# A four-layer hybrid trunk on one core: the heads of its FFNs written out by hand through their second block, with the weight sums on VectorE, and the last products of differential attention shared out between the pieces that follow them

## The chip, the core and the metric

One core of a Trainium2 chip runs the whole program in one launch. The core has five engines with queues of their own: TensorE (PE in the profile, its weight loads PEld), VectorE (DVE), ScalarE (ACT), GpSimd (POOL) and SyncE (SP), and 16 DMA engines that all of them share. The metric is the time of one execution in microseconds (us). For the kernel before, three runs took 2422.5 to 2428.01 us, median 2423.11.

## The reference, cut to what matters

`x` has 512 tokens of 1024 numbers in float32. Four layers follow each other; each adds a mixer and then an FFN to `x`. The mixers are S5, GLA, differential attention and S5 again.

```
for layer in range(4):
    h = rmsnorm(x, norm_mix[layer]);  x = x + mixer[layer](h)
    h = rmsnorm(x, norm_ffn[layer])
    g, u = split(h @ w_gate_up[layer])        # 1024 -> 2 x 2816
    x = x + (silu(g) * u) @ w_down[layer]     # 2816 -> 1024
```

Differential attention ends in `o @ w_o`, a product of 512 x 1024 by 1024 x 1024, which is added to `x`.

## The kernel before, in words

**Products in three parts.** Each float32 operand is split into a high part, rounded to a form that TensorE reads quickly (`F32R`), and a low part, the rest. A product is three matmuls: high by high, high by low, low by high. The high part is a copy on ScalarE (line 279 for weights, 185 for activations) and the low part a subtraction on VectorE that waits for it (280 and 186). `Trunk.halves` (276 to 281) does both for a weight piece of 128 x 1024 and writes a tile `whl`, of which there are 5.

**FFN of layers 1, 2 and 3** (`Trunk.ffn` and `seven_block`). The 2816 hidden columns are cut into 11 blocks of 256. In a block, gate and up together are a 2 x 2 block product: two halves of the tokens by two halves of the 1024 inputs, times two halves of the inputs by (gate, up). It is done with seven products instead of eight, in Winograd's form. The left operands, called sides, are `11`, `12`, `22`, which are quarters of the activations, and `1`, `2`, `3`, `4`, sums and differences of them (`Sides.total`, 191 to 205). The right operands are quarters of the weights: `11` and `21` (gate), `22` (up), and sums: `1` is up plus gate of the first input half, `3` is up of both halves. These two sums are made by DMA: a load from SP's queue (534 or 273), and then a second, accumulating load from GpSimd's queue (537), which waits until the first has landed. Later, `22` and then `21` are added onto `1` in place (`added`, 593, and the beginning of `four`, 613): on GpSimd for blocks 0 and 1, on VectorE for the others.

Each product is 24 matmuls of 128 x 256 (line 508). The steps of a block are `one` (sides `11`, weights `11`), `two` (`12`, `21`), `five` (`1`, `1`), `six` (`2`, `1` + `22`), `seven` (`3`, `3`), `three` (`4`, `22`), `four` (`22`, `1` + `22` + `21`). `one`, `six`, `seven` and `four` accumulate in the same PSUM bank `a`, so each waits until the one before has been copied or subtracted out (572, 600, 604, 546); `five` and `three` share bank `c`, `two` has `d`. The outcome is `act`, silu(gate) times up, again split (629, 630).

**Normalisation.** The sides are taken from `x` times the gain; the factor 1/rms of each token comes later. `Left.take` (78 to 92) multiplies by the gain (86), squares on ScalarE (98), and appends a transposition to the list `pend`, which `flush` empties one call later. `put` (103) transposes on TensorE (107) and `keep` (188) copies out. `finish` (116) makes 1/rms, with a power on GpSimd (125); `diag`, `spread` and `rows` (128 to 142) make of it a tile `R` that has the factor of each token in every row.

**Room.** The four quarters of the activations lie in `F`. When the sides have been built, each quarter's room takes weights of blocks 2 and 3 (`freed`). Other rooms are three `slots`, the gain's tile, and two `lent` rooms for the first two blocks' `1`. A staged weight goes to `wst`, of which there are 3.

**The head.** The first two blocks (a and b below) overlap the building of the sides. `Trunk.hand` switches the scheduler off: what is emitted then stands in each engine's queue as written. In `ffn` the steps from `split("21")` of block 0 up to `six` of block 1 are written by hand; the rest (`seven`, `three`, `four` of blocks 0 and 1, and all from block 2 on) is ordered by the scheduler. The loads of a block come in the order `11`, `21`, `1`, `22`, `3`, and rooms are handed out first in, first out. SP's queue and GpSimd's queue run their DMAs in order: one that waits holds those behind it.

After block 3, block 7 and block 10 a product with `w_down` (`gemm_b`, 294 to 296) adds to `x`. In layer 2, when block 2's loads have been issued, `turn_x` (737 to 748) writes `x` to memory and reads it back in another order of tokens, from GpSimd's queue; its results in `act` are written in two pieces (`turn`).

**The end of differential attention** (`diff`, up to 1990). Its product with `w_o` is made in two halves of 512 columns. The first half (`last`) runs between the heads' softmax work. Of the second, token tiles 0 and 1 run in two banks up to their last input tile, then `last` is emptied, then these two are finished, and then tiles 2 and 3. Each finished tile is added to `x` (438) and handed to `take`; each `take` first puts out the transposition that the one before left.

## Time and profile before

| | |
|---|---|
| median of three runs | 2423.11 us (2422.5 to 2428.01) |
| the profiled execution | 2425.78 us, of which its span is 2424.1 us |
| instructions | 35200 |
| TensorE busy | 2282.2 us, 94% of the span |
| VectorE, ScalarE, GpSimd busy | 1495.5, 1070.4 and 329.8 us |
| memory read, written | 275.92 MB, 23.99 MB |

How to read the rows that follow in the prediction. A row of the order of events has start and length in us, engine, line, operation, written tile and read tiles, their shapes, a count when equal instructions were merged, and in brackets how long the engine had been idle before and what ended that. `SPq` and `POOLq` are the queues that issue DMAs. A row of stretches has the stretch, its length, busy time of PE, PEld, DVE, ACT and POOL with counts, the granted TensorE clock as a share of full speed, the busy share of the DMA engines, and GB/s. A row of DMA issues has the tile, the count, the KB of each and the us from issue to landing.

### The profile page before, as it was taken

What the parts mean: (1) busy time and instruction counts of PE and PEld (TensorE: products, weight loads), DVE (VectorE), ACT (ScalarE), POOL (GpSimd) and SP (SyncE); (2) the same over time, 40 slices, a digit from 0 to 9 for tenths busy, and PEclk for the clock granted to TensorE, in tenths of its full rate; (3) what the DMA queues carried; (4) which work ended last, traced back from release to release, by engine and by line L of the source; (5) the groups of instructions that cost most, each with busy time, mean ns of one, the idle gap of its engine ahead of it and who ended that gap; (6) DMA issues with size and microseconds to landing.
All of it is one profiled execution on the core that took longest, in us unless ns stands there. A gap on an engine that the chain in (4) does not pass through costs nothing. (4 is left out here: it accounts for less than half of the span.)

```text
span 2424.1 us, 35200 instructions
## 1 busy us (share of the span) xinstructions
PE 2282.2 (94%) x14054; PEld 1975.2 (81%) x14054; DVE 1495.5 (62%) x2276; ACT 1070.4 (44%) x1740; POOL 329.8 (14%) x366
## 2 busy tenths in 40 slices
PE   4799999999999998999999998899999799899997
PEld 3578888788877788898987886798989688899996
DVE  7764655555433477484754676875856874867674
ACT  4453435444352355252534675553533233544442
POOL 4330100210100021010002131310000210301000
PEclk9799999999999999999999999999999899999999
DMA  4124343544432258574335465585732645666621
GB/s 111 32 50 139 101 148 126 165 132 155 135 96 70 83 135 207 131 180 118 105 127 121 106 143 153 145 231 125 186 90 85 210 160 142 166 173 142 172 72 69
DMA packets 275503, 317.42 MB, mean 131 GB/s; under 512 B 45653, under 2 KB 214377, under 8 KB 274058
## 3 DMA queue, kind: packets, MB, share of 16 engines
q1 hardware_dynamic: 227210, 238.14, 31.7%
q0 software_dynamic: 48128, 77.02, 15.4%
q8 instruction: 111, 1.82, 0.3%
q14 instruction: 54, 0.44, 0.1%
HBM read 275.92 MB, written 23.99 MB: 124 GB/s over the span
## 5 line engine op out<-in xcount | busy, mean ns | idle before, releaser
L280 DVE TENSOR_TENSOR whl<-wst,whl 128x1024 fp32r<-128x1024 f32 x294 | 359.9, 1226 | 367.8 <-ACT whl L279 365.0
L279 ACT CAST whl<-wst 128x1024 fp32r<-128x1024 f32 x294 | 308.7, 1052 | 531.5 <-PE acc L296 352.7
L508 PE MATMUL a<-side,whl 128*128 128x256 f32 x2376 | 301.5, 285 | 33.9 <-ACT r L600 26.9
L508 PEld LDWEIGHTS a<-side,whl 128*128 128x128 f32 x2376 | 290.7, 195 | 36.8 <-ACT r L600 28.1
L296 PE MATMUL acc<-whl,act 128*128 128x512 f32 x704 | 277.3, 394 | 0.0
L295 PE MATMUL acc<-whl,act 128*128 128x512 f32 x704 | 276.0, 392 | 0.0
L294 PE MATMUL acc<-whl,act 128*128 128x512 f32 x704 | 275.5, 391 | 0.0
L508 PE MATMUL c<-side,whl 128*128 128x256 f32 x1584 | 191.9, 277 | 0.2 <-DVE whl L280 0.2
L508 PEld LDWEIGHTS c<-side,whl 128*128 128x128 f32 x1584 | 186.3, 188 | 0.4 <-DVE whl L280 0.4
L295 PEld LDWEIGHTS acc<-whl,act 128*128 128x128 f32 x704 | 132.2, 188 | 29.4
L294 PEld LDWEIGHTS acc<-whl,act 128*128 128x128 f32 x704 | 132.2, 188 | 29.4 <-issue 0.7
L296 PEld LDWEIGHTS acc<-whl,act 128*128 128x128 f32 x704 | 132.3, 188 | 26.9
L294 PE MATMUL any<-hT,whl 128*128 128x512 f32 x384 | 151.7, 395 | 0.0
L295 PE MATMUL any<-hT,whl 128*128 128x512 f32 x384 | 149.6, 390 | 0.0
L296 PE MATMUL any<-hT,whl 128*128 128x512 f32 x384 | 149.6, 390 | 0.0
L294 PE MATMUL acc<-whl,hT 128*128 128x512 f32 x352 | 144.3, 410 | 2.0 <-DVE ro L1784 1.3
L295 PE MATMUL acc<-whl,hT 128*128 128x512 f32 x352 | 139.2, 395 | 0.9 <-DVE whl L280 0.9
L296 PE MATMUL acc<-whl,hT 128*128 128x512 f32 x352 | 139.4, 396 | 0.0
L280 DVE TENSOR_TENSOR whl<-halves,whl 128x1024 fp32r<-128x1024 f32 x60 | 73.4, 1224 | 67.7 <-ACT whl L279 67.4
L295 PE MATMUL acc<-whl,zT 128*128 128x512 f32 x256 | 103.9, 406 | 5.2 <-DVE whl L280 5.2
L294 PE MATMUL acc<-whl,zT 128*128 128x512 f32 x256 | 103.1, 405 | 2.7 <-ACT zT L410 2.7
L296 PE MATMUL acc<-whl,zT 128*128 128x512 f32 x256 | 103.6, 406 | 1.2 <-DVE zT L411 1.2
(425 smaller groups left out, 4253.4 us busy)
## 6 DMA issues: line engine op xcount, KB each, us to landing
wst<-in_ffn_w_gate_up_dram SPq DMA_DIRECT2D x110, 512.0 KB, 3.9
wst<-in_ffn_w_down_dram SPq DMA_DIRECT2D x88, 512.0 KB, 3.9
halves<-in_ffn_w_gate_up_dram SPq DMA_DIRECT2D x42, 512.0 KB, 4.7
slot<-in_ffn_w_gate_up_dram SPq DMA_DIRECT2D x39, 512.0 KB, 4.4
wst<-in_ffn_w_gate_up_dram POOLq DMA_DIRECT2D x33, 512.0 KB, 6.3
wst<-in_s_w_glu_dram SPq DMA_DIRECT2D x32, 512.0 KB, 3.7
spill<-opsp POOLq DMA_DIRECT2D x8, 2048.0 KB, 8.8
wst<-in_gla_w_in_dram SPq DMA_DIRECT2D x24, 512.0 KB, 3.6
```

Of the source, the lines that this page charges most:

```text
L279: nc.scalar.copy(hl[:, 0], w[:])
L280: nc.vector.tensor_tensor(hl[:, 1], w[:], hl[:, 0].bitcast(F32), op=ALU.subtract)
L294: mm(out, lh, rh, start=first, stop=False)
L295: mm(out, lh, rl, start=False, stop=False)
L296: mm(out, ll, rh, start=False, stop=last)
L508: mm(o, hl[:, x, k, c], side[:, y, k], start=first and not (j or k or n), stop=k == 3 and n == 2, skip_group_check=True,)
```

## The change

1. In `ffn`, the whole of blocks 0 and 1 up to their last products is now written by hand, as a list of words in which `:a` and `:b` are steps of block 0 and 1, a trailing `a` or `b` belongs to a split, a sum, a high or a low part of that block, and words without are those of the sides. `seven`, `three` and `four` are cut into a product and what follows it (`_out`). Splits can be written as high part (ScalarE) and low part (VectorE) apart.
2. The sums of `22` and `21` onto `1` are on VectorE for all blocks.
3. The loads of blocks from 2 on come in the order `11`, `1`, `22`, `21`, `3`, and the rooms of the sides are handed out in a new order, mixed with the slots.
4. The square of the last token tile and half is a step of the list (`square`); `r2` of block 1 has a tile of its own.
5. At the end of `diff`, `take` no longer flushes (`lazy`); the eight transpositions, the two additions of tiles 0 and 1, and the two early weight pieces (`ahead`) are put between the products of token tiles 2 and 3. `hand_all` is called there and in `gemm_b`, just ahead of `ahead`, no longer inside it.

```diff
@@ Left.take
-        tr.flush(1 - d)
-        if d and self.early:
+        if not tr.lazy:
+            tr.flush(1 - d)
+        if d and self.early and t < NT - 1:
             self.square(t, d)
...
@@ seven_block
-        def added():
-            (nc.gpsimd if b < 2 else v).tensor_tensor(W["1"][:], W["1"][:], W["22"][:], op=ALU.add)
+        def add(name):
+            v.tensor_tensor(W["1"][:], W["1"][:], W[name][:], op=ALU.add)
+            done(name) if name == "21" else None
...
         def four():
-            (nc.gpsimd if b < 2 else v).tensor_tensor(W["1"][:], W["1"][:], W["21"][:], op=ALU.add)
-            done("21")
-            self.seven_product(A["22"], W["1"], bank["a"], False)
+            product("22", "1", bank["a"], False)
             done("1")
+
+        def four_out():
             g2 = T("g2")
             scaled(g2, bank["a"], 1)
...
@@ ffn, instead of the calls for f[0], f[1] and left, one by one
+            plan = """
+                split21a one:a split21b square flush one:b total1 one_out:a finish high1 low1 total2 split1a high2 low2
+                one_out:b two:a two:b split1b high3 two_out:a five:a add22a highSa two_out:b lowSa five_out:a five:b
+                add22b highSb diag lowSb low3 split3a six:a spread five_out:b rows six:b six_out:a split3b seven:a
+                six_out:b total4 split22a high4 low4 seven:b seven_out:a split22b three:a seven_out:b gate1:a gate1:b
+                high22 low22 three:b add21a highFa add21b lowFa highFb lowFb four:a four:b three_out:a three_out:b
+            """
...
             self.hand()
-            slots += left.freed() + [left.g[:].rearrange("p (k n) -> p k n", n=256)]
+            F = left.freed()
+            slots[:] = [F[0], F[1], slots[0], F[2], left.g[:].rearrange("p (k n) -> p k n", n=256), F[3]] + slots[1:]
...
                     if n > 1:
-                        b["direct"]()
-                        b["roomed"]()
-                        b["rest"]()
-                        b["summed"]()
+                        for w in ("direct", "room1", "room22", "room21", "summed"):
+                            b[w]()
...
@@ diff
+            self.lazy = True
             run(last)
-            nxt[0].ahead(1)
+            self.hand_all()
             evac = self.add_x(1, nxt[0])
             for t in range(2):
                 unit(t, KT - 1)
-                evac(t, banks[t])
+            one = lambda: self.pend.pop(0)()
+            between = {
+                2: {1: (one,), 3: (one, lambda: evac(0, banks[0])), 5: (one, lambda: evac(1, banks[1])), 7: (one,)},
+                3: {1: (one,), 3: (one, lambda: nxt[0].ahead(1)), 5: (one,)},
+            }
             for t in range(2, NT):
                 banks.append(self.acc())
-                if t == 3:
-                    nxt[0].ahead(1)
                 for k in range(KT):
                     unit(t, k)
+                    for f in between[t].get(k, ()):
+                        f()
                 evac(t, banks[t])
+                if t == 2:
+                    nxt[0].ahead(1)
+            self.lazy = False
```

More of the change, by code (lines that the diff above doesn't have):

```diff
@@ L631, in four @@
             return act
[L633 to L637 removed]
+        return {f.__name__: f for f in (
+            high, low, split, direct, room21, room1, room22, summed, one, one_out, two, two_out, gate1, five, five_out,
+            add, six, six_out, seven, seven_out, three, three_out, four, four_out,
+        )}
     def ffn(self, l, left, after=None, turn=False, aside=None):
```

144 lines of the change are left out of this document (71 added, 73 removed).

## The prediction

> **What bounds the kernel now.** I read the busy table first, then the time by stages, then the order of events on TensorE where a stage has holes. TensorE (PE) is busy for most of the span, so time can only be won where it waits or where its clock is low.
>
> ```profile
> PE 2282.2 (94%) x14054; PEld 1975.2 (81%) x14054; DVE 1495.5 (62%) x2276; ACT 1070.4 (44%) x1740; POOL 329.8 (14%) x366
> ...
> 880.48:955.65 75.17, 64.02 (x519) 63.05 (x518) 63.69 (x67) 39.69 (x52) 20.65 (x11) 0.95 0.68 168
> 955.65:1100.00 144.35, 144.35 (x1049) 135.89 (x1048) 99.83 (x110) 66.93 (x82) 11.58 (x9) 1.00 0.63 162
> 1526.00:1606.78 80.78, 67.52 (x520) 66.53 (x518) 67.02 (x72) 44.08 (x59) 23.40 (x15) 0.90 0.77 202
> 2059.62:2134.04 74.42, 64.74 (x519) 63.58 (x518) 64.07 (x66) 41.17 (x53) 20.70 (x11) 0.93 0.68 170
> ```
>
> The rows after the first are stretches: length, busy time of PE, weight load, DVE, ACT and POOL, granted clock, DMA share, GB/s. Three are the FFN heads of layers 1, 2 and 3, from the first product of block 0 to the first of block 3; 955.65:1100 is what follows in layer 1, where PE is never idle. So block 3 onwards is PE's own pace and the heads are not: in each, PE idles for about 10 to 13 us and the clock is 0.90 to 0.95. The change touches just these and the stretch before 1526.
>
> ```profile
> 909.31 3.01 PE L508 MATMUL a<-side,whl 128*128 128x256 f32 x24 [3.26 <-ACT r L600]
> 929.18 5.49 PE L508 MATMUL a<-side,whl 128*128 128x256 f32 x24 [6.11 <-ACT r L600]
> 955.65 3.02 PE L508 MATMUL a<-sides,whl 128*128 128x256 f32 x24
> 975.01 0.39 PE L294 MATMUL acc<-whl,act 128*128 128x512 f32 x1
> ```
>
> Start, length, operation, and in brackets the wait before it. These are the two largest waits of head 1, 9.4 of its 11.1 us of idle time (75.17 less 64.02). The seven products of block 3 run from 955.65 to 975.01, 2.77 us each. So the 21 products of a head need 58.2 of its 75.2 us.
>
> **Why it waits.**
>
> ```profile
> 890.24 1.22 DVE L280 TENSOR_TENSOR whl<-lent,whl 128x1024 fp32r<-128x1024 f32 x1
> 892.87 3.13 DVE L280 TENSOR_TENSOR whl<-lent,whl 128x1024 fp32r<-128x1024 f32 x1 [0.21 <-ACT whl L279]
> 895.92 0.67 DVE L579 TENSOR_TENSOR r<-r,d 128x512 f32<-128x512 f32 x1
> 896.52 3.05 DVE L280 TENSOR_TENSOR whl<-lent,whl 128x1024 fp32r<-128x1024 f32 x1
> ...
> 900.09 3.05 DVE L280 TENSOR_TENSOR whl<-lent,whl 128x1024 fp32r<-128x1024 f32 x1
> 903.06 3.50 DVE L186 TENSOR_TENSOR side<-s,side 128x512 fp32r<-128x512 f32 x2
> 891.53 3.38 POOL L593 TENSOR_TENSOR lent<-lent,slot 128x1024 f32<-128x1024 f32 x1 [5.07 <-DVE whl L280]
> 907.72 0.37 SPq L534 DMA_DIRECT2D halves<-in_ffn_w_gate_up_dram  x1
> 913.06 1.28 POOL L537 DMA_DIRECT2D halves<-in_ffn_w_gate_up_dram  x1 [1.94 <-DMA halves<-in_ffn_w_gate_up_dram]
> 925.08 1.05 ACT L279 CAST whl<-halves 128x1024 fp32r<-128x1024 f32 x1 [7.16 <-DMA halves<-in_ffn_w_gate_up_dram]
> ```
>
> Two causes. A low part costs DVE 1.22 us, but 3.05 to 3.50 beside GpSimd's four weight sums, which makes the 3.26 wait. And block 2's summed quarter is loaded into the last side to come free (907.72), added at 913.06 and read only at 925.08: that is the 6.11. Layer 2 repeats both, and the stretch of layer 3 is alike.
>
> ```profile
> 1554.80 4.37 PE L508 MATMUL a<-side,whl 128*128 128x256 f32 x24 [3.34 <-ACT r L600]
> 1574.80 5.43 PE L508 MATMUL a<-side,whl 128*128 128x256 f32 x24 [5.86 <-ACT r L600]
> 1601.49 5.49 PE L508 MATMUL a<-side,whl 128*128 128x256 f32 x24 [3.21 <-DVE r L604]
> 1562.96 25.41 DMA gain<-in_ffn_w_gate_up_dram
> xturn<-vall POOLq DMA_DIRECT2D x1, 2048.0 KB, 27.0
> 904.00:912.00 8.00, 4.74 (x41) 4.54 (x40) 8.00 (x7) 4.70 (x7) 3.32 (x2) 1.00 0.67 209
> 1553.00:1561.00 8.00, 6.21 (x40) 6.21 (x41) 8.00 (x9) 7.19 (x9) 3.02 (x4) 0.79 0.92 262
> 1600.00:1608.00 8.00, 6.51 (x33) 6.51 (x34) 7.11 (x9) 3.88 (x5) 1.29 (x1) 0.57 0.90 217
> ```
>
> Layer 2 has a third wait of 3.21 us: block 3's quarter lies in the gain's room and lands after 25.4 us, beside the turn of x (27.0). Waits also cost clock: around 1553 and 1600 it is 0.79 and 0.57, which is 1.7 and 3.4 us in 8; around 904, at an equal wait, it is 1.00.
>
> **The change part by part.** *Sums to VectorE.* Each head loses four GpSimd sums and gains four of 1.14 us on DVE (the pace of such pieces: 886.64 less 885.50 in the rows of L205 and L132, length 1.22). It loses 1.9, 1.8 and 1.8 us of blocked low parts and 2.2 in the two of 903.06 (1.3 when free, as two 512-wide pieces): 7.8 out, 4.6 in. DVE works 63.7 - 3.2 = 60.5 us in a head. GpSimd's queue then has only r and the accumulating DMAs, which no longer stand behind sums.
>
> *Order and rooms.* Block 2's summed quarter now goes into the first side to come free, after the second total (about 9 us into the head instead of 27), and nothing but r is ahead of its accumulation. By the rows above, 5.3 us for the load and 12 for the sum, it is there at about 26, and wanted at 46: the 6.11 and 5.86 waits lose this cause by 20 us. Block 3's quarter follows at 28 instead of 37 or later. SP is passed too: the two staged loads now stand ahead of the second side and wait for block 0's and 1's third quarter, at 23 to 25 us; the side behind them is free at 25, so this is free of charge.
>
> *What is late next.* I laid the new written order of PE, DVE and ACT with the paces of the rows, start to start: product 2.77, DVE 1.14 (1024 wide) and 0.60 (512: 895.92 to 896.52), ACT 0.95, 0.48 (a copy) and 0.53 (silu). A hand-over takes 0.14 (891.78 + 0.95 to 892.87), and 0.3 behind PE, whose product rows are 0.25 longer than their pace.
>
> ```profile
> 885.50 1.22 DVE L205 TENSOR_TENSOR halves<-halves 128x1024 f32<-128x1024 f32 x1
> 886.64 0.87 DVE L132 TENSOR_SCALAR diag<-ident,rcol 128x128 f32<-128x128 f32 x4
> 889.62 1.05 PE L138 MATMUL rows<-diag,ones 128*128 128x128 f32 x8
> 891.78 1.05 ACT L279 CAST whl<-lent 128x1024 fp32r<-128x1024 f32 x1
> 908.68 0.58 ACT L600 COPY r<-a 128x512 f32<-128x512 f32 x1
> 909.15 1.05 ACT L185 CAST side<-halves 128x1024 fp32r<-128x1024 f32 x1
> 910.11 0.63 ACT L547 ACTIVATE r<-r 128x512 f32<-128x512 f32 x1
> 910.64 1.04 ACT L279 CAST whl<-wst 128x1024 fp32r<-128x1024 f32 x1
> ```
>
> PE then runs twelve products, `one:a` to `three:b`, with transposes and row sums (1.2) and 0.4 for slower first products, without a wait, to 34.9 us. The first wait is `four:a`: after `seven:b` (29.4) come 0.3, its subtraction and two gate products on DVE (1.8), two silu and a high part on ACT (2.0), then on DVE the side's low part, two sums and a low part (4.6), hand-overs 0.2: 38.2, while PE has two products in stock. **3.3 us of wait.** Behind it block 2: eight pieces of 0.6 and a low part stand on DVE ahead of its `five`: 1.1; sum, high and low of its `six`: 1.35; low of `two`: 0.9. Together 6.7, so block 3 begins at 66.4 instead of 75.2. The table load for silu in layers 2 and 3 falls into ACT's wait for the gate: nothing (1.3 if that cover goes).
>
> For the clock I take one loss of 1.7 us a head, because the 3.3 is like the waits of 1554.80 and 1601.49, which were slowed, and 909.31, which was not; 1.7 is the smaller of the two losses seen. Bounds 0 and 3.4. So layer 1 wins 75.2 - 68.1 = **7.1**, layer 3 74.4 - 68.1 = **6.3**.
>
> *Layer 2* splits its activations into four low parts of 0.53 per block, not two.
>
> ```profile
> 1573.13 2.12 DVE L630 TENSOR_TENSOR act<-r,act 128x256 fp32r<-128x256 f32 x4
> ```
>
> Three more stand ahead of block 2's `five`: 1.7 us with a hand-over, and that wait becomes about 3, for which I take 0.9 more of clock. From `one:b` on I get 63.4 (66.4 less 3.3 for `one:a` and a transpose, and 0.3 because DVE comes later) + 1.7 + 1.7 + 0.9 = 67.7, against 77.5 from 1529.30 to 1606.78: **9.8**. The turn of x starts some 6 us sooner and competes with loads. If block 3's quarter, issued at 28 us, again takes 25.4 and its sum 12, it is there at 65; it is wanted at 69. That cover of 4 us is thin.
>
> *End of attention.*
>
> ```profile
> 1508.03 1.41 PE L107 MATMUL tp<-ident,hh 128*128 128x128 f32 x8 [1.04 <-DVE hh L86]
> 1512.30 1.09 PE L107 MATMUL tp<-ident,hh 128*128 128x128 f32 x4 [2.16 <-DVE hh L86]
> 1529.30 1.91 PE L508 MATMUL a<-sides,whl 128*128 128x256 f32 x14
> 1510.00:1516.00 6.00, 3.84 (x14) 3.17 (x14) 3.33 (x5) 3.09 (x8) 0.00 (x0) 0.72 0.93 196
> ```
>
> Before, transposes wait 1.04 and 2.16 us and the clock loses 1.7 (0.28 of 6): 4.9. After, each follows six products (1.4 us). Three still wait: the third for the copy of the first (0.25), the fifth for the copy of the third, which on ACT stands behind a square that waits for a low part on DVE (1.5), and the last, behind DVE's two low parts and the differences for side 3 (1.15). Of 4.9 won, 2.9 return: **2.0**, bounds 0 and 4.9.
>
> Sum: 7.1 + 6.3 + 9.8 + 2.0 = 25.2. The profiled execution took 2425.8 (span 2424.1), which gives 2400.6; the median of the runs is 2423.1, and from it comes **2398**.
>
> **A rule against a row.** The Trainium skill, "TensorE: Matmul & The Clock Gate", section "The HAM clock gate", says that the clock halves after at least one idle window of about 3.4 us. The trace does not bear this out strictly: 3.34 and 3.21 us, and 2.16 with transposes beside it, already cost clock. What the rule would give is a rival.
>
> **The rivals.**
> *The clock stays up.* The remaining waits of 3.3 us and less slow nothing, as at 909.31: 1.7 + 1.7 + 2.6 = 6.0 more won: 2392. The page named above would have it so. Against: two of the three quoted waits of 3.2 to 3.4 us were slowed. Chance 0.20.
> *Layer 2 is bound by its transfers.* Its DMA share is 0.77 already, and 0.92 from 1553 to 1561; squeezed into 12 us less it is 0.9. If block 3's sum comes 10 us past its time, layer 2 wins nothing: 2408. Chance 0.15.
> *The wait moves.* Block 2's quarter lands late in all heads, so that 6.1 us and 3.4 of clock remain there in place of 1.1: 8.4 a head, 25 in all: 2423. From 9 to 46 us it has 37; the load and sum of block 2 took 17 in layer 1, the load of block 3 alone 25 in layer 2. Chance 0.07.
> *VectorE's hand-written queue becomes the bound: slower.* One DVE instruction waiting for ACT holds all behind it, and each of 19 low parts waits for a high part, each sum's high part for the sum. Idle DVE time in head 1 is now 11.5 us (75.2 less 63.7); 60.5 + 11.5 is 72. From 14.7 us of idle time on, a head is longer than before; at 0.95 us, a whole high part, for each of the 19 it is 18, and the head 78.5: 3.3 a head longer, 2433. Chance 0.06.
> That the change does not do what it says I exclude: in its instruction order the sums are on DVE and products alternate a, b to `four`.
>
> **How the numbers follow.** Forecast 2398 with 0.52; the rivals above 0.20, 0.15, 0.07 and 0.06. A difference of 0.3%, 7 us, is about what a measurement of this kernel can tell from no change. Faster by more than that: 0.52 + 0.20 + 0.15 less 0.01 = 0.86; within: 0.08; slower: 0.06. The range leaves out the two last rivals: below, the clock rival with the attention term at its bound, 2389, and 2 more for timing errors of my paces, 2387; above, the transfer rival and 4 for longer hand-overs, 2412.
>
> **What would show it.** Low parts at 1.2 us all through the heads, and four DVE sums each; no wait on PE before `four:a`, then one of about 3.3 us released by a DVE low part; block 2's `five` released by DVE, not by a DMA's ACT read; head lengths of 68 us; clock 1.00 or 0.8 behind that wait; in layer 2 the load into the fifth room long before its sum is wanted. I am wrong if ACT waits for a DMA inside a head, or DVE idles over 14 us in one.

## The result, and the profile after

The kernel after takes 2392.14 us (median of four runs, 2391.18 to 2402.76); the kernel before took 2422.81 beside it (2418.9 to 2428.01). The ratio is 0.9882, with a 95% interval from 0.9849 to 0.9916: between 20 and 37 us are won, 31 by the medians. The prediction said 2398 with a range of 2387 to 2412.

The first view is the busy table of the kernel after.

```profile
PE 2269.0 (95%) x14054; PEld 1962.3 (82%) x14054; DVE 1485.4 (62%) x2288; ACT 1070.3 (45%) x1740; POOL 293.3 (12%) x354
```

TensorE is busy 13 us less with the same 14054 instructions, so part of what was won is slow clock; the rest is waiting. The next view has the stretches of the kernel after: the head of layer 1, the head of layer 2, its block 3, and the head of layer 3. Columns as in the prediction.

```profile
875.82:941.04 65.22, 62.06 (x520) 61.44 (x518) 59.64 (x69) 40.65 (x53) 8.78 (x7) 0.97 0.74 187
1502.12:1572.09 69.97, 62.77 (x517) 61.51 (x516) 64.62 (x77) 44.56 (x60) 11.90 (x12) 0.98 0.86 226
1572.09:1599.24 27.15, 21.58 (x170) 21.39 (x169) 16.26 (x20) 10.81 (x16) 2.15 (x2) 0.87 0.87 228
2033.85:2099.44 65.59, 62.44 (x519) 61.71 (x518) 60.04 (x70) 42.00 (x54) 8.81 (x7) 0.97 0.73 187
```

The heads of layers 1 and 3 are 9.95 and 8.83 us shorter (75.17 and 74.42 before). In layer 2 the stretch from the second product to block 3 is 12.6 shorter (64.88 after, 77.48 before), but then block 3 itself, which took 19.6 before, takes 27.2. That is the surprise of this profile.

To weigh layer 2 as a whole I use one stretch with the same end points in every kernel: from a matmul shortly ahead of the first transposition at the end of attention to one in the middle of the first product with `w_down`. First before, then after.

```profile
1503.20:1663.48 160.28, 143.69 (x938) 131.92 (x937) 114.35 (x128) 77.17 (x109) 31.05 (x21) 0.94 0.71 178
```

```profile
1483.98:1637.88 153.90, 139.45 (x938) 127.49 (x936) 110.85 (x132) 77.34 (x109) 19.19 (x17) 0.97 0.74 186
```

So the end of attention and layer 2 together win 6.4 us. With 9.95 and 8.83 that makes 25.2 us in the stretches that the change touches. The two profiled executions (2425.78 and 2391.65) lie 34.1 apart; the other 9 stand in stretches where both kernels issue the same instructions in the same order (4.7 ahead of the head of layer 1, 4.6 between that layer's FFN and the end of attention). The first product of layer 1's head, for instance, begins at 880.48 before and at 875.82 after, and in the twelve runs below it begins anywhere from 874.78 to 882.03. So a few us between two kernels are read here from stretches, and not from one execution's whole time.

Where TensorE still waits in the head of layer 1 (order of events, kernel after):

```profile
905.09 5.60 PE L523 MATMUL c<-side,whl 128*128 128x256 f32 x48
912.65 0.50 PE L523 MATMUL a<-side,whl 128*128 128x256 f32 x2 [1.96 <-ACT whl L291]
913.91 7.12 PE L523 MATMUL a<-side,whl 128*128 128x256 f32 x46 [0.76 <-DVE whl L295]
920.87 3.02 PE L523 MATMUL a<-sides,whl 128*128 128x256 f32 x24
923.73 2.90 PE L523 MATMUL c<-side,whl 128*128 128x256 f32 x24
927.32 0.51 PE L523 MATMUL d<-sides,whl 128*128 128x256 f32 x2 [0.43 <-ACT whl L291]
```

The first row is `three:a` and `three:b`, the next two `four:a` and `four:b`, then block 2's `one`, `five` and the first two matmuls of its `two`. The wait ahead of `four:a` is 2.72 us in two parts, first for the high part of its weights, then for the low part. The 46 matmuls behind it take 7.12 us: the clock is low for part of them. Of the 6.11 us that block 2 waited for its quarter nothing is left. The cause is seen in the queues of SP and GpSimd, kernel after:

```profile
884.92 0.37 SPq L556 DMA_DIRECT2D halves<-in_ffn_w_gate_up_dram  x1
888.92 1.31 POOL L559 DMA_DIRECT2D halves<-in_ffn_w_gate_up_dram  x1 [6.28 <-ACT side L212]
```

The load is issued 9.1 us into the head and the accumulating load at 13.1; before, they were at 27.2 and 32.6.

The new wait in layer 2 is in block 3. The rows are of the kernel after: two of TensorE, two of ScalarE, one of SP's queue, one piece of the chain of waits, and the landing times of the tile `wst` from 1500 to 1600.

```profile
1583.42 4.95 PE L523 MATMUL a<-side,whl 128*128 128x256 f32 x24 [5.57 <-ACT r L595]
1602.75 0.50 PE L308 MATMUL acc<-whl,act 128*128 128x512 f32 x1 [1.28 <-DVE g L568]
...
1579.51 1.04 ACT L291 CAST whl<-wst 128x1024 fp32r<-128x1024 f32 x1 [6.94 <-DMA wst<-in_ffn_w_gate_up_dram]
1582.74 0.62 ACT L595 COPY r<-a 128x512 f32<-128x512 f32 x1
...
1545.01 2.27 SPq L281 DMA_DIRECT2D wst<-in_ffn_w_gate_up_dram  x1
...
1570.27 9.14 DMA wst<-in_ffn_w_gate_up_dram
...
DMA to landing us min/median/max: 3.5/6.5/24.7
```

Read from the bottom: the load of block 3's quarter `3`, issued at 1545.01, is the one that took 24.7 us. Its accumulating load could start only at 1570.27 and took 9.14. The high part of that quarter (1579.51) stands in ScalarE's queue ahead of the copy that empties block 3's `one` (1582.74), so `six`, which accumulates into the same bank, waits 5.57 us and then runs at low clock (4.95 us instead of 2.88). The product that needs the quarter, `seven`, comes two products later. A transfer that was late for one engine's queue has stopped a product that does not use it.

### The profile page after: what moved, and what is told of

Read it like the earlier page. It is cut to its first block, busy times and chain, and to the rows that moved or that the text cites. A ratio compares the mean times of both kernels' runs of the same rounds, so it can differ in the third digit from the quotient of the medians.

```text
span 2389.9 us, 35198 instructions
## 1 busy us (share of the span) xinstructions
PE 2269.0 (95%) x14054; PEld 1962.3 (82%) x14054; DVE 1485.4 (62%) x2288; ACT 1070.3 (45%) x1740; POOL 293.3 (12%) x354
## 5 line engine op out<-in xcount | busy, mean ns | idle before, releaser
L523 PE MATMUL a<-side,whl 128*128 128x256 f32 x2376 | 294.7, 281 | 15.0 <-ACT whl L291 6.4
L523 PEld LDWEIGHTS a<-side,whl 128*128 128x128 f32 x2376 | 284.7, 192 | 17.0 <-ACT whl L291 7.2
L309 PE MATMUL acc<-whl,zT 128*128 128x512 f32 x256 | 104.3, 407 | 5.7 <-DVE whl L295 5.7
L295 DVE TENSOR_TENSOR whl<-halves,whl 128x1024 fp32r<-128x1024 f32 x72 | 87.8, 1223 | 32.6 <-ACT whl L291 32.5
L291 ACT CAST whl<-halves 128x1024 fp32r<-128x1024 f32 x72 | 75.4, 1053 | 69.8 <-PE acc L310 26.7
L308 PE MATMUL acc<-whl,zT 128*128 128x512 f32 x256 | 103.3, 406 | 2.7 <-ACT zT L425 2.7
```

What stands on the lines that cost most here:

```text
L291: self.nc.scalar.copy(hl[:, 0], w[:])
L295: self.nc.vector.tensor_tensor(hl[:, 1], w[:], hl[:, 0].bitcast(F32), op=ALU.subtract)
L308: mm(out, lh, rh, start=first, stop=False)
L309: mm(out, lh, rl, start=False, stop=False)
L523: mm(o, hl[:, x, k, c], side[:, y, k], start=first and not (j or k or n), stop=k == 3 and n == 2, skip_group_check=True,)
```

## The experiments

Each row of this table is a kernel run against the kernel before on the same chip. "Head 1" and "head 3" are the heads of layers 1 and 3 and "stretch 2" is the stretch from the end of attention into the first product with `w_down`, in us, from one profiled execution each. The rows are not all from one chip, so ratios compare two of them better than medians.

| kernel | median | ratio to before (95%) | head 1 | head 3 | stretch 2 |
|---|---|---|---|---|---|
| before | 2422.81 | 1 | 75.2 | 74.4 | 160.3 |
| after | 2392.14 | 0.9882 (0.9849 to 0.9916) | 65.2 | 65.6 | 153.9 |
| e1, after, sums on GpSimd | 2397.09 | 0.9896 (0.9874 to 0.9917) | 66.2 | 66.3 | 154.3 |
| e2, before, sums on VectorE | 2392.87 | 0.9897 (0.9867 to 0.9927) | 65.8 | 66.1 | 148.9 |
| e3, after, old rooms and loads | 2400.99 | 0.9913 (0.9894 to 0.9932) | 65.3 | 65.5 | 159.6 |
| e4, after, old end of attention | 2398.11 | 0.9904 (0.9879 to 0.9929) | 65.0 | 65.1 | 154.3 |
| e5, after, turn of x later | 2393.87 | 0.9888 (0.9868 to 0.9907) | 65.1 | 65.4 | 154.1 |
| e6, after, no turn of x | 2388.13 | 0.9860 (0.9841 to 0.9879) | 66.3 | 65.5 | 144.4 |
| e7, after, side 22 ahead of gate1 | 2389.16 | 0.9867 (0.9849 to 0.9886) | 63.8 | 63.3 | 151.5 |
| e9, after, VectorE's order filled | 2393.29 | 0.9883 (0.9862 to 0.9905) | 63.2 | 63.2 | 156.1 |
| e10, before, new load order alone | 2399.74 | 0.9912 (0.9896 to 0.9927) | 69.5 | 67.9 | 156.5 |
| e11, e7 and split turn | 2387.98 | 0.9865 (0.9843 to 0.9887) | 63.8 | 63.4 | 147.2 |
| e12, e11 and diag on ScalarE | 2391.69 | 0.9881 (0.9863 to 0.9898) | 64.2 | 64.2 | 150.0 |
| e13, e9 and split turn | 2385.53 | 0.9864 (0.9843 to 0.9886) | 63.2 | 63.2 | 148.4 |

Head 1 is the same code in after, e4, e5 and e6 and took 65.0 to 66.3 us. So under about 1 us between two heads, each from one execution, says little; most of that spread goes with the clock, as shown further down.

### Which part takes the 10 us from a head?

**e1: the sums back on GpSimd.**

```diff
-            v.tensor_tensor(W["1"][:], W["1"][:], W[name][:], op=ALU.add)
+            (nc.gpsimd if b < 2 else v).tensor_tensor(W["1"][:], W["1"][:], W[name][:], op=ALU.add)
```

> The kernel after, with the four sums of each head (22 and 21 onto 1 for blocks 0 and 1) put back on GpSimd; orders and rooms as after. Theory A, the place of the sums carries much of the gain: the low parts beside the sums take 3.05 us again instead of 1.22 and each high part waits for a longer sum, so blocks 0 and 1 of a head take 48 to 52 us instead of 45.1 and the kernel some 15 us more, 2407. Rival B, the written order alone did it: blocks 0 and 1 stay within 1 us of 45.1, and the kernel within 3 us of 2392.

The head of layer 1, one sum on GpSimd, and two rows of VectorE beside it (e1):

```profile
876.12:942.28 66.16, 61.87 (x519) 60.32 (x518) 62.15 (x65) 40.70 (x53) 19.64 (x11) 1.00 0.74 185
886.37 3.39 POOL L616 TENSOR_TENSOR lent<-lent,slot 128x1024 f32<-128x1024 f32 x1 [3.43 <-DVE whl L295]
887.71 3.14 DVE L295 TENSOR_TENSOR whl<-lent,whl 128x1024 fp32r<-128x1024 f32 x1 [0.20 <-ACT whl L291]
894.34 3.15 DVE L133 TENSOR_SCALAR diag<-ident,rcol 128x128 f32<-128x128 f32 x4
```

The low part is slow again (3.14 us), yet the head is only 0.94 us longer, and head 3 0.69. For layers 1 and 3 rival B is right: with the new order the place of the sums hardly matters. VectorE loses the sums (4.6 us) and gains blocked time, 62.15 us of work against 59.64, but idles 4.0 us in head 1 instead of 5.6. Blocks 0 and 1 took 44.6 us, not 48 to 52. In layer 2 it is otherwise: the head takes 79.2 us instead of 70.0, and block 3 behind it 19.9 instead of 27.2, so that stretch 2 hardly changes. The kernel at 2397.09 lies 5 us above 2392, outside the 3 of rival B, but the intervals overlap. The Trainium skill, "SBUF — State Buffer", section "SBUF: two separate sides", says that GpSimd and an operation of VectorE with two inputs in SBUF take a shared port by an exclusive lock, so that the later one blocks altogether. The rows agree: the sum ends at 889.76, and the low part that had begun at 887.71 ends 1.09 us after that, about the time of a free one.

**e2: the kernel before with the sums on VectorE, and nothing else.**

```diff
-            (nc.gpsimd if b < 2 else v).tensor_tensor(W["1"][:], W["1"][:], W["22"][:], op=ALU.add)
+            v.tensor_tensor(W["1"][:], W["1"][:], W["22"][:], op=ALU.add)
...
-            (nc.gpsimd if b < 2 else v).tensor_tensor(W["1"][:], W["1"][:], W["21"][:], op=ALU.add)
+            v.tensor_tensor(W["1"][:], W["1"][:], W["21"][:], op=ALU.add)
```

> The kernel before with one edit: the four sums of each head are on VectorE; order, rooms and loads as before. Theory A, by the prediction's step (7.8 us of blocked low parts go, 4.6 us of sums come, the 3.26 us wait goes): each head 3 to 4 us shorter, with the 6.1 us wait for block 2's quarter still there; the kernel about 10 us below before. Rival B, from the run with the sums on GpSimd (heads only 0.7 to 0.9 us longer in layers 1 and 3): where the sums stand matters little as long as the rest of the order is that of before, within 1.5 us a head, within 5 us of before.

Neither theory: two lines of the change give its whole gain, as far as the intervals tell. The first two rows are the head of layer 1 and stretch 2 of e2, the others the load of block 2's quarter, its accumulating load, and the first read.

```profile
876.61:942.36 65.75, 61.14 (x520) 59.94 (x519) 60.06 (x70) 39.52 (x52) 9.69 (x7) 1.00 0.71 185
1484.86:1633.72 148.86, 138.85 (x937) 126.31 (x936) 111.14 (x132) 76.17 (x109) 20.06 (x17) 0.99 0.76 193
901.26 0.37 SPq L534 DMA_DIRECT2D halves<-in_ffn_w_gate_up_dram  x1
905.41 1.31 POOL L537 DMA_DIRECT2D halves<-in_ffn_w_gate_up_dram  x1 [22.82 <-ACT whl L279]
916.04 1.04 ACT L279 CAST whl<-halves 128x1024 fp32r<-128x1024 f32 x1 [1.37 <-DMA halves<-in_ffn_w_gate_up_dram]
```

I had expected the 6.11 us wait for block 2's quarter to stay, because rooms and load order are the old ones. It went. Without blocked low parts the sides end sooner, the room comes free 24.7 us into the head instead of 27.2, GpSimd's queue has no sum in it, so the accumulating load follows at 28.8 instead of 32.6, and the quarter is read at 39.4 instead of 44.6. With the old load order the late quarter was a result of the slow low parts, not a second cause beside them. In layer 2 these two lines do better than the whole change: block 3 takes 20.2 us, with the turn of `x` behind block 2's loads as in after, and stretch 2 is 5.0 us shorter than in after. By stretches e2 wins 29.2 us (9.4, 8.3 and 11.4) and the whole change 25.2; by whole times the two can't be told apart.

**e10: the kernel before with the new load order, and nothing else.**

```diff
+        def one_first():
+            load("1", 0, 1, (0, 0))
+            load("22", 1, 1)
+            load("21", 1, 0)
...
-                        b["roomed"]()
-                        b["rest"]()
+                        b["one_first"]()
```

> The kernel before with one edit: blocks from 2 on are loaded in the order 11, 1, 22, 21, 3, so that block 2's summed quarter takes the first side's room that comes free. Sums on GpSimd, written order and rooms as before. Theory A, each of the three parts of the change (sums, written order, rooms) is enough by itself to take most of the 10 us from a head, since what is left is VectorE's own work: the 6.11 and 5.86 us waits go, heads of layers 1 and 3 take 67 to 69 us (VectorE works 63.7 of them, with the blocked low parts still in), layer 2 from its second product to block 3 about 70; kernel 2400 to 2405. Rival B, the rooms bring nothing, as the undone rooms in the kernel after cost layers 1 and 3 nothing: heads within 1.5 us of before, kernel 2418 to 2424.

```profile
876.05:945.58 69.53, 62.59 (x519) 61.70 (x518) 64.89 (x66) 39.86 (x52) 20.56 (x11) 0.98 0.73 182
```

Theory A for layers 1 and 3: an early quarter alone is worth 5.6 us in head 1 and 6.5 in head 3, with the sums still on GpSimd and VectorE busy for 64.89 of the 69.53 us.

**e3: the kernel after with the old rooms and load order.**

```diff
-            slots[:] = [F[0], F[1], slots[0], F[2], left.g[:].rearrange("p (k n) -> p k n", n=256), F[3]] + slots[1:]
+            slots[:] = F + [left.g[:].rearrange("p (k n) -> p k n", n=256)] + slots
...
-                        for w in ("direct", "room1", "room22", "room21", "summed"):
+                        for w in ("direct", "room21", "room1", "room22", "summed"):
```

> The kernel after, with the load order of before for blocks from 2 on (11, 21, 1, 22, 3) and the rooms handed out as before (the four quarters, the gain's room, then the slots). Theory A, the new rooms took away the 6.11 us wait of block 2: block 2 of layers 1 and 3 takes 25 to 26 us instead of 20.2 and 20.4, the kernel about 15 to 18 us more, 2409. Rival B, the earlier end of the sides does it as well: the side's room comes free at 903.9 in layer 1, 5.3 us of load and 12 of sum give 921.4, and the quarter is wanted at 923.7, so layers 1 and 3 stay within 1 us, and only layer 2 with its slow transfers loses up to 5: 2392 to 2397.

Rival B: heads 1 and 3 stay (65.3 and 65.5), and layer 2 loses 5.7. The kernel at 2400.99 is 4 us above rival B's range and far under theory A's 2409. So a head of layers 1 and 3 is shortened by the sums (8.3 to 9.4 us alone), by the load order (5.6 and 6.5 alone), and by the written order with the new rooms and the sums on GpSimd (8.1 to 9.0); the written order alone was not run. Together they give 8.8 to 9.95. They do not add: something else ends the head once one of them is there.

### What is the floor of a head?

VectorE works 59.6 us in a head of after, and 60.1 in e2. Three runs test whether its queue is the floor.

**e7: side 22 and the sums of 21 ahead of gate1** in the written order.

```diff
-                ... seven_out:b gate1:a gate1:b high22 low22 three:b add21a highFa add21b lowFa highFb lowFb four:a
+                ... seven_out:b high22 low22 three:b add21a highFa add21b lowFa highFb lowFb gate1:a gate1:b four:a
```

> The kernel after with two gate steps moved in the written order: high and low part of side 22 and the two sums with their parts come ahead of gate1 of both blocks, so that the side's high part does not stand behind two silu on ScalarE. The 2.7 us wait ahead of the product four of block 0 should fall to under 0.5 in all heads, and blocks 0 and 1 to 41 to 42 us. Theory A, VectorE's queue sets the end of the head: block 2 then takes 21.5 to 22.5 us where it took 20.2 to 21.5, since its waits of 1.1 and 1.3 us come back, and a head is 1 to 2 us shorter (the 1.6 us for which VectorE idled). Rival B, waits and clock add up as in the prediction: block 2 unchanged, heads 3 to 4.5 us shorter.

```profile
875.99:939.80 63.81, 61.71 (x519) 61.31 (x518) 59.42 (x69) 40.72 (x53) 8.78 (x7) 0.97 0.77 195
910.70 5.95 PE L523 MATMUL a<-side,whl 128*128 128x256 f32 x48
921.78 4.40 PE L523 MATMUL c<-side,whl 128*128 128x256 f32 x22 [2.03 <-DVE whl L295]
```

`four:a` (910.70) no longer waits, and blocks 0 and 1 take 40.5 us instead of 45.05. But block 2's `five` now waits 2.03 us for a low part, and its matmuls run at low clock, where it had not waited at all. The heads win 1.4 and 2.3 us, and block 2 takes 23.3 and 22.6. That is theory A, with sizes a little over its own: the product was waiting for its turn in VectorE's queue, and taking one wait away moves it to the next product.

**e9: the written order filled up on VectorE.**

```diff
-                one_out:a finish high1 low1 total2 split1a high2 low2 one_out:b two:a two:b split1b high3 two_out:a ...
+                one_out:a finish high1a high1 low1a low1 total2 high1b high2 low1b low2 one_out:b two:a two:b high3 ...
...
-                ... split3b seven:a ... seven:b seven_out:a split22b three:a seven_out:b gate1:a gate1:b high22 low22 ...
+                ... split3b add21a seven:a ... seven:b high22 low22 add21b seven_out:a split22b three:a seven_out:b ...
```

> The kernel after with the written order of the head filled up on VectorE: parts of 1 for both blocks ahead of or between the first two side sums, the sums of 22 ahead of the low parts that wait for ScalarE, side 22 and the sums of 21 between seven and its subtractions, gate1 last. No instruction more or less. Theory A, VectorE's queue sets the end of the head: its idle time in a head falls from 5.6 us to about 2.5, and heads of layers 1 and 3 are 3 us shorter (62 to 62.5 us); layer 2, bound by its transfers, wins under 1 us up to the end of its first product with w_down. Rival B, TensorE with its waits and clock is the bound: the heads are 4.5 us shorter, as in the run that only moves gate1, and no better than that run.

Heads 1 and 3 take 63.2 us, 2.0 and 2.4 less than after and at most 0.6 less than e7. That is under the 3 us of theory A and far under the 4.5 of rival B, and VectorE still idles 4.35 and 3.86 us, where 2.5 were expected: the new order did not fill it as meant, so this run alone does not decide. In layer 2 what the head wins is lost again: block 3 takes 31.4 us there, 27.2 in after.

**e12: diag on ScalarE**, on top of e11.

```diff
-            nc.vector.tensor_scalar(diag[:, t], tr.ident[:], self.r[:, t : t + 1], None, op0=ALU.mult)
+            if self.early:
+                nc.scalar.mul(diag[:, t], tr.ident[:], self.r[:, t : t + 1])
+            else:
+                nc.vector.tensor_scalar(diag[:, t], tr.ident[:], self.r[:, t : t + 1], None, op0=ALU.mult)
```

> The kernel of the split turn, and in the three heads diag (four pieces, 0.87 us together) on ScalarE instead of VectorE. Theory A, VectorE's queue sets the end of a head: heads of layers 1 and 3 are 0.5 to 0.9 us shorter than with the split turn alone. Rival B, the path runs through TensorE and ScalarE there, and VectorE has room at that place: within 0.2 us, or longer if ScalarE comes late with the parts behind diag.

```profile
900.32 1.27 ACT L134 ACTIVATE diag<-ident,rcol 128x128 f32<-128x128 f32 x4
900.45 1.23 DVE L298 TENSOR_TENSOR whl<-lent,whl 128x1024 fp32r<-128x1024 f32 x1 [1.17 <-ACT whl L294]
904.96 1.23 DVE L298 TENSOR_TENSOR whl<-wst,whl 128x1024 fp32r<-128x1024 f32 x1 [0.95 <-ACT whl L294]
1587.23 4.54 PE L526 MATMUL a<-side,whl 128*128 128x256 f32 x24 [4.19 <-ACT r L598]
```

The heads are 0.4 and 0.8 longer, not shorter: rival B. (In head 3 part of that is clock, 0.97 against 1.00 in e11; in head 1 it is 0.97 in both.) VectorE lost about 0.8 us of work (58.65 us in head 1 after 59.45), but the low part behind the missing diag waits 1.17 us for ScalarE (0.39 in e11) and a later one 0.95 (0.65), since diag's 1.27 us now stand ahead of that high part. So VectorE's work alone is not the floor. Its queue with the hand-overs from ScalarE fits all three runs; that no path past VectorE is as long was not shown. The last row is block 3 of layer 2 and is taken up with e11.

### Does a slow clock cost its own length?

Runs e4 and e5 have the heads of layers 1 and 3 of the kernel after, and so has e6; what differs there is the clock. The first four rows are the head of layer 1 in e5, the same product `four` with the same wait as in the kernel after, and block 2's `five`; the last is `four` in the head of layer 1 of e6.

```profile
875.66:940.77 65.11, 61.29 (x520) 60.26 (x518) 59.42 (x69) 40.82 (x53) 8.76 (x7) 1.00 0.76 190
912.49 0.50 PE L523 MATMUL a<-side,whl 128*128 128x256 f32 x2 [1.95 <-ACT whl L291]
913.75 5.68 PE L523 MATMUL a<-side,whl 128*128 128x256 f32 x46 [0.76 <-DVE whl L295]
923.18 2.79 PE L523 MATMUL c<-side,whl 128*128 128x256 f32 x22 [0.64 <-DVE whl L295]
...
919.54 8.19 PE L523 MATMUL a<-side,whl 128*128 128x256 f32 x46 [0.58 <-DVE whl L295]
```

In e5 the clock stayed at 1.00 and the 46 matmuls take 5.68 us instead of 7.12: 1.44 us saved. The head is 0.11 us shorter. Block 2's `five`, which did not wait in the kernel after, waits 0.64 here, and block 2 takes 21.5 us instead of 20.2; blocks 0 and 1 took 43.6 instead of 45.05. In the kernel after the slow clock had given VectorE the time to catch up, so the first 1.44 us of slow clock and the later waits are nearly one and the same loss. The other heads agree: with full clock they take 65.0 to 65.1 us (e4 twice, e5), with one slow stretch 65.2 to 65.6 (heads 1 and 3 of after, head 3 of e5 and of e6). In e6's head 1 the clock was low for longer, the 46 matmuls took 8.19 us, and block 2 the same 20.2 as in after; the 1.07 us that go beyond 7.12 made the head 1.07 longer. So a slow clock is free only up to the length of the waits that it replaces.

### What holds layer 2?

**e4: the end of attention as before**, heads as after.

```diff
-            self.lazy = True
             run(last)
             self.hand_all()
+            nxt[0].ahead(1)
             evac = self.add_x(1, nxt[0])
             for t in range(2):
                 unit(t, KT - 1)
+                evac(t, banks[t])
...
             for t in range(2, NT):
                 banks.append(self.acc())
+                if t == 3:
+                    nxt[0].ahead(1)
                 for k in range(KT):
                     unit(t, k)
-                    for f in between[t].get(k, ()):
-                        f()
                 evac(t, banks[t])
-                if t == 2:
-                    nxt[0].ahead(1)
             self.lazy = False
```

> The kernel after, with the end of differential attention as before (both additions and all transposes in their old places, the heads as after). Theory A, the end of attention is a gain of its own: the second product of layer 2's head begins 2 to 3 us later (2.0 by the prediction, 2.9 between the traces of before and after), the kernel at 2394 to 2395. Rival B, what is won there is lost again at the first side sums of the head: within 1 us of 2392. In both the head from its second product on stays at 64.9.

```profile
1492.82:1647.10 154.28, 141.49 (x937) 129.79 (x936) 111.23 (x132) 77.43 (x109) 19.20 (x17) 0.96 0.75 185
1501.92 0.63 PE L108 MATMUL tp<-ident,hh 128*128 128x128 f32 x4 [2.16 <-DVE hh L86]
```

The old end costs 1.45 us up to the head's second product and 1.2 more up to block 3 (66.1 instead of 64.9, which both theories had wrong). But at the end of stretch 2 only 0.4 us is left of it, 154.28 against 153.90: layer 2 gives the rest back. The 2.9 us between the traces of before and after hold 1.4 us of slow clock besides: in e4 the same waits of 1.04 and 2.16 us were followed by full clock (0.63 us for the four transpositions, 1.09 before), and in e2, which has the old end too, the second product comes just as early as in e4. The kernel at 2398.11 is above both theories, but its interval overlaps that of after.

**e6: no turn of x.**

```diff
-                    if turn and n == 2:
+                    if turn and n > 99:
```

> The kernel after without the turn of x in layer 2: its four transfers are left out and x keeps its order of tokens (so what follows works on other numbers; all else is as after). Theory A, the turn's 4 MB are what binds layer 2's transfers: block 2 at 22 to 23 us (its first wait is VectorE's), block 3 at 19.3, no wait in the first product with w_down, so layer 2 up to that product's end 8 to 9 us shorter; kernel about 2384. Rival B, the weights alone bind them: block 3 still over 23 us, less than 4 us won.

```profile
1490.19:1634.56 144.37, 136.79 (x938) 125.55 (x936) 110.78 (x132) 77.45 (x109) 16.46 (x13) 0.99 0.70 169
```

Block 3 takes 19.4 us, no wait is left in it or in the product with `w_down`, and stretch 2 is 9.5 us shorter: theory A. Without the turn's transfers the wait is gone. They do not make it alone: e2 has them, and its block 3 takes 20.2.

**e5: the turn behind block 3's loads.**

```diff
-                    if turn and n == 2:
+                    if turn and n == 3:
```

> The kernel after, with the turn of x in layer 2 issued after block 3's loads instead of block 2's. Theory A, the turn's 4 MB delay the quarter for block 3's product 3 (its load took 24.7 us and its sum 9.1, and a wait of 5.6 us with slow clock behind it came of that): block 3 of layer 2 takes 19.3 to 21 us instead of 27.0, the kernel 2385. Rival B, the transfers as a whole are the bound (busy share 0.86 from 1502 to 1572): the wait comes at another place (block 4, or the first product with w_down, which then waits for x), and the kernel stays within 2 us of 2392.

```profile
1487.65:1641.71 154.06, 139.84 (x938) 126.98 (x936) 110.64 (x132) 77.19 (x109) 19.11 (x17) 0.98 0.76 186
1604.36 0.50 PE L308 MATMUL acc<-whl,act 128*128 128x512 f32 x1 [3.46 <-DVE g L568]
1600.38 1.04 ACT L291 CAST whl<-wst 128x1024 fp32r<-128x1024 f32 x1 [4.69 <-DMA wst<-in_ffn_w_down_dram]
```

Block 3 falls to 22.7 us, and the product with `w_down` then waits 3.46 and runs at low clock behind it: 154.06 against 153.90. Rival B, with the wait at another place: now ScalarE waits for weights of `w_down` (4.69 us in the last row), VectorE for ScalarE, and the product for VectorE.

**e11: the turn in two steps**, on top of e7. The write to memory stays behind block 2's loads, the read back goes behind block 3's.

```diff
-                            r = self.turn_x(left.r)
+                            self.turn_out(left.r)
+                    if turn and n == 3:
+                        with self.tc.issue_after(self.added.ins):
+                            r = self.turn_in()
```

> The kernel with side 22 ahead of gate1 (e7), and in layer 2 the turn of x in two steps: the write after block 2's loads as before, the read back after block 3's loads. Theory A, the read back (2 MB) competes with block 3's last load and its sum, and ScalarE's queue, which holds a high part of that sum, stands: block 3 of layer 2 falls from 25.9 us to 20 to 21, the first product with w_down does not wait over 2 us, layer 2 is 5 us shorter and the kernel 2384. Rival B, the transfers as a whole are the bound: the 5.6 us reappear in the first product with w_down or in block 4, and the kernel stays at 2389.

```profile
1490.18:1637.33 147.15, 138.16 (x938) 126.80 (x936) 110.58 (x132) 77.19 (x109) 19.16 (x17) 0.98 0.78 194
```

Block 3 takes 20.5 us (26.0 in e7) and the stretch 147.15 (151.51 in e7): 4.4 us, close to the 5 of theory A; the product with `w_down` still waits 2.2. The read back waits for the write in any case; put behind block 3's last sum, it no longer stands in that sum's way. In the total only 1.2 us of this are seen (2387.98 after 2389.16), less than the intervals tell apart. And e12, with the same split turn, waits 4.19 us in block 3 (its last row above), takes 25.4 us for it, and its stretch 2 is only 1.5 us shorter than e7's.

**e13: the edits of e9 and of the split turn together.**

> The filled order of e9 together with the split turn of e11. Theory A, the two parts are independent: heads of layers 1 and 3 take 63.2 us as in e9, block 3 of layer 2 falls from 31.3 us to 20 to 22 as in e11, and layer 2 from its second product to the end of block 3 takes 83 to 85 us (93.8 with e9, 84.2 with e11); kernel 2385 to 2388. Rival B, what is won in layer 2's head only brings the first product of block 3 sooner to transfers that land when they land: layer 2 stays over 88 us and the kernel at 2390 to 2393.

```profile
874.78:937.93 63.15, 61.04 (x519) 60.22 (x518) 58.89 (x70) 40.67 (x53) 9.69 (x7) 1.00 0.76 195
1483.51:1631.89 148.38, 138.07 (x937) 126.81 (x936) 110.26 (x132) 77.74 (x109) 20.04 (x17) 0.98 0.78 193
```

The heads are as in e9, and stretch 2 falls from 156.1 to 148.4, but block 3 still takes 25.1 us, and from the second product to the end of block 3 it is 87.7: between the 83 to 85 of theory A and the 88 of rival B. At 2385.53 us (2382.6 to 2386.09) this kernel has the lowest median of all; its ratio, 0.9864, is that of e11, 0.9865. Its stretches beat those of after by 2.1, 2.4 and 5.5 us. Its interval against the kernel before (0.9843 to 0.9886) still overlaps that of after, so by whole times alone the gain over after isn't settled.

## Why the prediction was right, and where it was not

The time was right: 2398 forecast, 2392 measured, inside the range and with the sign that had 0.86. By stretches the sum is right as well, 25.2 us forecast and 25.2 measured. But it is right as a sum of terms that miss both ways, and the medians moved by 30.7: the 5.5 us more lie, as far as the profiled executions tell, outside the stretches of the change, and no term of the prediction stands for them.

| step | forecast | measured |
|---|---|---|
| head of layer 1 | 7.1 | 9.95 |
| head of layer 3 | 6.3 | 8.83 |
| layer 2, from the second product on | 9.8 | 12.6 up to block 3, then 7.5 lost in block 3 and 1.5 at the product with `w_down`: 3.5 |
| end of attention | 2.0 | 2.9 at the second product |

**Sums to VectorE.** Right in its rows: low parts take 1.22 us all through a head and VectorE works 59.6 us (60.5 said). Wrong as one term among several. The prediction gave the first wait to the sums and the 6.11 us to the rooms. e2 and e10 show that either edit takes most of the loss away, and e3 that in layers 1 and 3 the rooms bring nothing once the sums and the order are there.

**The first wait.** Right: none ahead of `four:a`, then 2.72 us there (3.3 said), 1.96 for the high part and 0.76 for VectorE's low part behind it, in all three heads.

**The waits of block 2 and the clock.** This is the step that failed. I added 1.1, 1.35 and 0.9 us of waits in block 2 to 1.7 of lost clock. The clock was low in all three heads, as said, but layers 1 and 3 then waited only 0.43 and 0.44 us. e5 shows why: the slowed products of `four` are time in which VectorE goes on, and with the clock up the later waits come back at nearly the same length, 1.33 us for the 1.44 saved. Two losses behind each other on TensorE, both caused by one late queue, cost the larger of the two and not their sum. Without the 1.7, the forecast of the heads would have been 8.8 and 8.0, against 9.95 and 8.83. The waits of block 2 were also too large by themselves: with full clock (e5) block 2 takes 21.5 us, 2.1 more than block 3, where I had summed 3.35.

**Layer 2.** The 12.6 against 9.8 is of the same kind: block 2's waits were 2.8 us (1.54, 0.49 and 0.76) where I had 5 to 5.3, and the clock was low in `four` alone, where I had 0.9 more for block 2. What followed is the rival "bound by its transfers", with another transfer: not block 3's quarter `1`, whose cover I had called thin, but its quarter `3`, the last load in SP's queue, and by way of ScalarE's queue. The end of attention and layer 2 together won 6.4 us of 11.8. e6 shows that without the turn of `x` the wait is gone, and e2 that with the old heads and load order the turn does no such harm.

**The end of attention.** 2.9 against 2.0 at the place where I counted it, and 0.4 where it matters (e4). The 4.9 us to be won had 1.7 of slow clock in them, and e4 and e2 show that the same waits can pass without it; there the new end is worth 1.45 at that place. So the nearness of 2.9 to 2.0 is in part luck.

**The rivals.** "The clock stays up" gave 2392, the measured time, but its mechanism did not come: the clock fell in all three heads. And where it did stay up (e4, e5), the head was 0.1 to 0.5 us shorter, not 1.7. "The wait moves" and the slower rival did not come either: in the head of layer 1 neither ScalarE nor VectorE waits for a transfer, and VectorE idled for 5.6 us of 65.2, far under the 14.7 at which a head would have become longer.

**What stays open.** Why block 3 of layer 2 still waits about 4 us in e12 and e13, which have the split turn of e11, when it waits 0.9 in e11, was not tried. With one execution of each, the 20.5 us of e11 may owe something to chance.

## What to carry to other kernels

Before parts of a change are priced one by one, ask whether they shorten the same queue: here two lines had the whole gain, and the rest of the change, which without them shortens a head by 8 to 9 us, added half a microsecond at most to what a head of layers 1 and 3 wins, and cost 5 in layer 2. A wait on TensorE and a slow clock behind it are not added when one late queue causes both: the larger counts. And a stretch that is won ahead of a bundle of transfers is only won when those transfers land sooner too; look for what is late next in the queue of the engine that reads them, where a late read also holds what does not need it.

## What the runs showed of the hardware

The clock can fall after a wait that is clearly shorter than the 3.4 us of the rule that the prediction quoted. In the kernel after, 1.96 and 0.76 us of wait with two matmuls between them were followed by a low clock in all three heads; the same wait, 1.95 and 0.76, was followed by full clock in layer 1 of e5. The rows are stretches, three of after and three of e5:

```profile
908.34:911.75 3.41, 2.35 (x21) 2.15 (x20) 2.64 (x3) 0.93 (x2) 0.00 (x0) 1.00 1.17 248
911.75:915.17 3.42, 1.76 (x12) 1.56 (x13) 3.39 (x4) 3.31 (x4) 0.85 (x1) 1.00 1.09 364
915.17:918.58 3.41, 3.41 (x19) 3.41 (x17) 3.40 (x6) 1.11 (x2) 0.45 (x1) 0.50 1.13 319
...
908.45:911.86 3.41, 2.09 (x19) 1.89 (x17) 2.92 (x3) 0.93 (x2) 0.00 (x0) 1.00 1.16 262
911.86:915.27 3.41, 2.02 (x15) 1.82 (x16) 3.38 (x4) 3.29 (x4) 1.29 (x1) 1.00 1.09 366
915.27:918.69 3.42, 3.42 (x32) 3.42 (x31) 3.42 (x6) 1.12 (x3) 0.81 (x1) 1.00 1.15 302
```

In the clock records of all 14 traces the clock changes only at points of a grid 3.41 us wide, which lies elsewhere against the program in each execution; the stretches are cut at these points. In after, 1.06 and 1.66 us of the idle time fall into two steps of the grid, and the step behind the second runs at half clock; in e5 it is 1.32 and 1.39, and no step is slow. In the FFNs of layers 1 to 3 of all 14 traces, no step at full clock with less than 1.66 us of idle time was followed by a slow one, and each with more than 1.79 was. So here about half a step of idle time costs the clock of the next step, and whether a wait of 1.7 to 3.4 us does so hangs on where the grid cuts it. That is why of two nearly equal waits in the prediction's rows one was slowed and one was not: at 909.31 the steps hold 1.55 and 1.70 us of idle time, at 1554.80 one holds 2.07.

The Trainium skill, "TensorE: Matmul & The Clock Gate", section "The HAM clock gate", also says that the window is free-running, and that where the clock changes depends on where in it the first matmul lands. The traces agree with that; 3.4 us as the least length of a wait that costs clock they do not bear out.

Beside a sum on GpSimd not only operations with two tensors are slow on VectorE: the four pieces of diag, with one tensor and a scalar per partition, took 3.15 us in e1 (894.34), where a sum on GpSimd ran from 894.50 to 897.00, and 0.87 before where nothing ran beside them.
